# Two-layer diffusion backbone on one core: second layer's values with a column of ones, work taken off VectorE, output gate folded into the weights, first token tiles finished in an earlier turn

## The chip, the cores and the metric

The kernel runs on one core of a Trainium2 chip. The metric is the device time of one launch in microseconds (us). The instructions run on five engines: TensorE (PE in the profile; its weight loads are PEld), VectorE (DVE), ScalarE (ACT), GpSimd (POOL), and SyncE (SP), whose queue issues the DMA transfers.

## The reference

Two layers of a diffusion backbone over 1024 latent tokens and 256 context tokens of width 1024, and a final RMSNorm:

```python
for i in range(DEPTH):                                   # DEPTH = 2
    hx = rms_norm(x, norm_g[i]) * (1.0 + sc_x) + sh_x    # sh, sc, g: modulation from silu(c) @ w_mod[i]
    hc = rms_norm(ctx, norm_g[i]) * (1.0 + sc_c) + sh_c
    ...                                                  # layer 0: GQA, QK norm, rotary; layer 1: below
    x = x + g_x * yx
```

Layer 1 is a neighbourhood attention with 16 heads of width 64. A token sees a window of 8 rows by 16 columns of the 16 x 64 grid with a learned bias, and all context tokens:

```python
px = hx @ w_in                                           # q, k, v, z, each 1024 wide
s = concat([q @ k_window * ATTN_SCALE + bias, q @ k_ctx * ATTN_SCALE])
p = softmax(s)
o = p[..., :n_nb] @ v_window + p[..., n_nb:] @ v_ctx
yx = (o * silu(z)) @ w_out
```

The last layer gives no context output. The result is `rms_norm(x, final_norm_g)`.

## The kernel before, in words

**Precision.** Every product of two float32 matrices is done in float16 parts: a high part and a remainder of each factor (a "split"), and three matmuls (high x high, high x low, low x high). A split is a ScalarE copy to float16 and a VectorE or POOL subtraction.

**Stages.** Until about 136 us the modulation vectors are computed while weights arrive. Then comes layer 0 with its attention (names with a: `pa`, `pv`, `poa` are PSUM tiles of its projections, its weighted values and its out-projection), to about 774 us. Token tiles have 128 tokens: 0 to 7 are latent, 8 and 9 are context (NX = 8, NT = 10). Tile t's output is gated (`tm`, VectorE), added to the stream (`x1`, L1358, POOL) and handed to `ln_pair`, which normalises two tiles at once (`x16`, `x17` are tiles 6 and 7) and prepares layer 1's input.

**Entry of layer 1.** Its projections use a fast block multiplication (Winograd's form of Strassen: 7 block products for 8, `winograd`). So its factors are sums and differences of blocks, on the tokens' side made in `ln_pair` (L704 to L707: POOL, VectorE, POOL, VectorE) from the halves of a pair of tiles. The float16 rows before these sums are `hrb6a` for tiles 6 and 7, and after them `hrb6s` (`0` high, `1` low). DMA transposes them into `hx`. On the weights' side `b_load` forms the block sums (`wtb`, four POOL operations per weight tile, L1429 to L1432), and ScalarE and VectorE split them (`wb`, L1434, L1435). The products land in `pwq0a` to `pwq7c` (queries and keys of head pairs 0 to 7) and `pwv0a` to `pwv7c` (values and gates).

**Attention of layer 1.** `b_att(u)` works on head pair u: for each of 2 heads and 8 token tiles, scores over the near tiles and the context, a maximum, four exponentials (two into float16 `ph`, two into float32 `pf`, whose sums go into `bsm`), the remainder by `p_split` (every fourth on VectorE, L1127; the others as two halves on POOL, L1130), a DMA transposition into `bpht`, and then two matmuls per key tile (L1642 over 128 columns: values' high and low part at once; L1644 over 64). Per head and four tiles, `fin` (L1653 to L1660) makes the reciprocal of the sums, adds the two parts, scales and multiplies with the gate path `bsz`.

**Out-projection.** `b_part` multiplies with w_out; pairs 0 to 5 (K1 = 6) run during the last pair's attention, pairs 6 and 7 in `b_out(t)` (PSUM tiles `pob<t><half>6`). Each half-tile is multiplied with the gate (L1751, VectorE, `tmb`) and added to the residual `acc` (L1752, POOL, for tile 7 in `b_out` VectorE). Then `b_out` squares (L1760, ScalarE), takes the reciprocal root (L658 VectorE, L660 POOL) and scales (L1765, VectorE).

**What sets the order.** The program is written in the order that `timeline` makes from start and end values given to each part: of the live parts it takes a step of the one whose next step has the lowest value. Then `Planner` reorders each engine's instructions over the whole program, by a list schedule with its own costs and by due times derived from TensorE's order. So a change of one line can move instructions far from it.

## Time and profile before

| | us |
|---|---|
| median of three runs (lowest, highest) | 1360.35 (1357.03, 1361.37) |
| profiled execution | 1362.21 |
| its span | 1360.3 |
| busy: TensorE, VectorE, ScalarE, POOL | 1309.5, 1129.6, 976.2, 909.9 |

The mean granted clock of TensorE in the profiled execution is 0.991 of full. A busy time is the time in which at least one instruction of an engine was in flight. What is idle is told in the rows by the wait in square brackets and by what ended it.

### The profile page before, as it was taken

Reading aid. Unit: us, or ns where it says so; the run is one execution under the profiler, and the core shown is the slowest. Engines: PE = TensorE matmul, PEld = TensorE weight load, DVE = VectorE, ACT = ScalarE, POOL = GpSimd, SP = SyncE. Lnnn points to the kernel's source line nnn. Section 1 sums busy time; section 2 is a strip of 40 time slices with the busy share of each in tenths; the row PEclk is TensorE's granted clock in tenths of the full one; section 3 lists DMA queues with packets and bytes.
Section 4 is the critical chain, followed back from the end, with each engine's and each line's share of the span. In section 5 each row is a group of like instructions: output and inputs, shape, how many; then the busy total and the mean of one; then the engine's idle time right before and its main releaser. Section 6 shows DMA issues by size and latency. Waiting matters only on the chain.

```text
span 1360.3 us, 37879 instructions
## 1 busy us (share of the span) xinstructions
PE 1309.5 (96%) x14492; PEld 923.2 (68%) x14492; DVE 1129.6 (83%) x2603; ACT 976.2 (72%) x2325; POOL 909.9 (67%) x1251
## 2 busy tenths in 40 slices
PE   8999999999999999999999899999999999999994
PEld 4467777777777777776654357868677686876551
DVE  5898687978898787769448898899999999999668
ACT  4654889888888777788733355897978889787443
POOL 2323778777777767788775566586676778755565
PEclk9999999999999999999999999999999999999997
DMA  9634566787874222245237953587677768679953
GB/s 368 186 114 114 118 125 144 153 153 146 141 142 104 66 77 60 57 118 139 79 109 175 219 109 90 115 151 146 121 142 151 150 130 173 126 165 257 262 113 124
DMA packets 390350, 191.58 MB, mean 141 GB/s; under 512 B 349776, under 2 KB 355088, under 8 KB 390168
## 3 DMA queue, kind: packets, MB, share of 16 engines
q1 hardware_dynamic: 389592, 189.13, 61.6%
q8 instruction: 113, 1.85, 0.6%
q14 instruction: 69, 0.57, 0.1%
q10 hardware_dynamic: 576, 0.03, 0.0%
HBM read 91.03 MB, written 15.75 MB: 78 GB/s over the span
## 4 chain that ended last, share of the span: by engine, by line
PE 49%; DVE 24%; ACT 11%; issue 6%; DMA 5%; POOL 4%; DVEq 0%; POOLq 0%; SPq 0%; ACTq 0%
PE pa L1034 12%; PE pob L1747 5%; PE st L1260 3%; PE st L1261 3%; DVE wb L1435 3%; PE pm L1068 3%; PE poa L1353 2%; PE pv L1137 2%; PE pv L1136 2%; PE pv L1138 2%; DVE bpf L1613 2%; DVE bk L1504 2%; DVE bmx L1620 2%; ACT bpf L1633 1%; ACT bph L1631 1%
## 5 line engine op out<-in xcount | busy, mean ns | idle before, releaser
L1130 POOL TENSOR_TENSOR pl<-pf,ph 128x256 f16<-128x256 f32 x400 | 274.8, 712 | 83.3 <-ACT pf L1247 59.0
L1130 POOL TENSOR_TENSOR bph<-bpf,bph 128x256 f16<-128x256 f32 (+1 forms) x192 | 167.5, 889 | 119.0 <-ACT bpf L1633 98.7
L1034 PE MATMUL pa<-wa,x 128*128 128x256 f16 x1536 | 219.3, 272 | 1.0 <-DVE q L822 1.0
L1245 ACT ACTIVATE ph<-st 128x512 f16<-128x512 f32 x240 | 143.2, 602 | 56.4 <-PE st L1261 55.1
L1560 PEld LDWEIGHTS <-hx 128*128 128x128 f16 x2688 | 156.7, 98 | 11.7 <-issue 4.9
L1034 PEld LDWEIGHTS <-x 128*128 128x128 f16 x1536 | 139.7, 97 | 33.2 <-DVE q L822 1.3
L1247 ACT ACTIVATE pf<-st 128x512 f32<-128x512 f32 x240 | 143.2, 603 | 1.9 <-POOL pl L1130 1.2
L1069 DVE TENSOR_REDUCE mxp<-pm 128x1 f32<-128x512 f32 x192 | 127.5, 683 | 16.2 <-PE pm L1068 15.1
L1137 PE MATMUL pv<-v,ph 128*128 128x64 f16 x960 | 122.5, 195 | 0.0
L1136 PE MATMUL pv<-v,ph 128*128 128x65 f16 x960 | 122.1, 193 | 0.0
L1138 PE MATMUL pv<-v,pl 128*128 128x65 f16 x960 | 121.5, 192 | 0.4 <-POOL pl L1130 0.4
L1512 PEld LDWEIGHTS <-wb 128*128 128x128 f16 x672 | 63.5, 99 | 81.2 <-issue 10.9
L1130 POOL TENSOR_TENSOR qpp<-qpf,qpp 128x256 f16<-128x256 f32 (+1 forms) x158 | 94.2, 621 | 33.8 <-ACT qpf L1203 25.7
L1631 ACT ACTIVATE bph<-bpf,bnx 128x384 f16<-128x384 f32 (+1 forms) x128 | 69.9, 581 | 55.7 <-DVE bnx L1623 35.6
L1136 PEld LDWEIGHTS <-ph 128*128 128x128 f16 x960 | 90.7, 96 | 23.2 <-DVE og L1118 1.7
L1137 PEld LDWEIGHTS <-ph 128*128 128x128 f16 x960 | 90.3, 97 | 14.4 <-issue 0.4
L1138 PEld LDWEIGHTS <-pl 128*128 128x128 f16 x960 | 91.1, 99 | 9.4 <-POOL pl L1130 1.1
L1260 PE MATMUL st<-q,k 128*128 128x512 f16 x240 | 90.9, 379 | 1.9 <-ACT pf L1247 1.2
L1261 PE MATMUL st<-q,k 65*128 65x512 f16 x240 | 91.2, 381 | 0.0
L1353 PE MATMUL poa<-woa,oa 128*128 128x512 f16 x384 | 89.7, 379 | 0.0
L1747 PE MATMUL pob<-wob,obf 128*128 128x512 f16 x336 | 79.9, 379 | 0.2 <-DVE tmb L1751 0.2
L1633 ACT ACTIVATE bpf<-bpf,bnx 128x384 f32<-128x384 f32 (+1 forms) x128 | 74.4, 581 | 0.2
(486 smaller groups left out, 4045.6 us busy)
## 6 DMA issues: line engine op xcount, KB each, us to landing
wg<-in_w_mb SPq DMA_DIRECT2D x32, 512.0 KB
wsb<-in_b_wp SPq DMA_DIRECT2D x64, 256.0 KB
wm<-in_w_m SPq DMA_DIRECT2D x16, 512.0 KB
wsa<-in_a_wq SPq DMA_DIRECT2D x32, 256.0 KB
xstage<-in_x SPq DMA_DIRECT2D x8, 512.0 KB
wsoa<-in_a_w_out SPq DMA_DIRECT2D x16, 256.0 KB
x<-in_x SPq DMA_DIRECT2D x8, 512.0 KB
x_d<-x SPq DMA_DIRECT2D x8, 512.0 KB
```

Source lines behind the costliest of these rows:

```text
L1034: T.matmul(ps[:, :, i, :], hA(a, kt, t), wt[w][:, kt, :], start=n == 0, stop=n == 3 * KT - 1)
L1069: V.tensor_reduce(mxs[i][:, t, ch:ch + 1], pm, axis=AX.X, op=ALU.max)
L1130: G.tensor_tensor(lo[:, c], p32[:, c], hi[:, c], op=ALU.subtract)
L1136: T.matmul(pv[:, t, :], hi[:, c], v[:, 0:65], start=first and t == 0, stop=False)
L1137: T.matmul(pv[:, t, 0:HD], hi[:, c], v[:, 65:129], start=False, stop=False)
L1138: T.matmul(pv[:, t, :], lo[:, c], v[:, 0:65], start=False, stop=last and t == n - 1)
L1245: S.activation(ph, st, AF.Exp)
L1247: S.activation(p32, st, AF.Exp)
L1260: T.matmul(so, k1[:, g, kc], q1[:, :, i, :], start=True, stop=False)
L1261: T.matmul(so, k2[0:65, g, kc], q2[0:65, :, i, :], start=False, stop=True)
L1560: T.matmul(ps[:, t * P:(t + 1) * P], hx[a][:, t, blk, kt], wt[j][:, s_, w, kt], start=first and t == 0 and m == 0, stop=last and t == 3 an ...
L1747: T.matmul(ps, ob[kt][:, t, a], wout["b"][hf][b][:, kt, :], start=n == 0, stop=n == 3 * len(kts) - 1)
```

## The change

1. `p_split` in layer 1 gives every eighth remainder to VectorE instead of every fourth (BEV 4 to 8): 16 of 128 move to POOL, two instructions each.
2. `ln_pair`: of the four block sums three are now on VectorE and one on POOL, with one sign turned (`scalar_tensor_tensor` with -1). To keep the products right, the weights' blocks come in another order and `BLK` points to other blocks.
3. `load_wout` multiplies the second layer's w_out with the gate on POOL when a weight tile arrives (16 tiles of 128 x 512), so `b_part` adds from PSUM into `acc` on VectorE in one instruction; the gate tile of before and the POOL additions go.
4. The addition of `x1` for tile 7 of the first layer is on VectorE.
5. `b_load` forms its block sums with three POOL operations, one of them over 256 columns, instead of four.
6. The values of layer 1 have a column of 2*WS*WS beside the high part (tile 130 wide, set by a POOL memset per head pair). The exponentials no longer sum, and a key tile takes three matmuls of 65, 64 and 65 columns, with the denominator in column 64 of the result.
7. `fin` becomes `o_evict`, which the first layer uses too: a reciprocal from PSUM, a scaling in PSUM, a product with the gate path.
8. The copy of the queries in `put` (L1501, VectorE) is a second ScalarE write from PSUM.
9. In `b_out` the first half of tiles 0 to 6 is scaled on ScalarE and multiplied with the norm weight on POOL.
10. The parts have other values for their turn: the last pair's attention ends at u + 0.6, and `b_out(t)` starts at 7.61 (t < 4) or 7.65, plus 0.09 t, instead of 8.01 + 0.1 t.

```diff
-BEV, BLAG = 4, 4
+BEV, BLAG = 8, 4
...
-        G.tensor_tensor(b2, b1, b2, op=ALU.add)
-        V.tensor_tensor(b1, a1, b1, op=ALU.subtract)
-        G.tensor_tensor(a1, b2, a1, op=ALU.subtract)
+        V.scalar_tensor_tensor(b2, b1, -1.0, b2, op0=ALU.mult, op1=ALU.subtract)
+        G.tensor_tensor(b1, a1, b1, op=ALU.subtract)
+        V.scalar_tensor_tensor(a1, b2, -1.0, a1, op0=ALU.mult, op1=ALU.subtract)
         V.tensor_tensor(a2, a2, a1, op=ALU.subtract)
...
+                    if gate is not None:
+                        G.tensor_tensor(st, st, gw, op=ALU.mult)
                 load_w(w, f, kt, 1, 512, f"o{nm}{kt}{hf}")
...
-            G.tensor_tensor(x1[:, hc], x1[:, hc], tm, op=ALU.add)
+            (V if t == NX - 1 else G).tensor_tensor(x1[:, hc], x1[:, hc], tm, op=ALU.add)
...
-            G.tensor_tensor(t1, b12, b11, op=ALU.subtract)
-            G.tensor_tensor(t2, b22, t1, op=ALU.subtract)
-            G.tensor_tensor(t3, b22, b12, op=ALU.subtract)
+            G.tensor_tensor(tt[:, 0:2], st[:, 1:3], b12.unsqueeze(1).broadcast_to([P, 2, P]), op=ALU.subtract)
+            G.tensor_tensor(t2, b22, t1, op=ALU.add)
             G.tensor_tensor(t4, b21, t2, op=ALU.subtract)
...
-        v1_ = bq.tile([P, NT, 2, P], F16, name=f"bv1{u}", tag="v1")
+        v1_ = bq.tile([P, NT, 2, 130], F16, name=f"bv1{u}", tag="v1")
+        G.memset(v1_[:, :, :, HD:HD + 1], 2.0 * WS * WS)
...
-                    V.tensor_copy(ov[0][oth, i, ts], ov[0][own, i, ts])
+                    S.activation(ov[0][oth, i, ts], src, AF.Copy, scale=sc)
...
-                        S.activation(pf[:, 0:n], pf[:, 0:n], AF.Exp, bias=m, accum_out=sums[:, t % 4, 0:1])
-                        S.activation(pf[:, n:n + 2], cx_, AF.Exp, bias=m, accum_out=sums[:, t % 4, 1:2])
+                        S.activation(pf[:, 0:n], pf[:, 0:n], AF.Exp, bias=m)
+                        S.activation(pf[:, n:n + 2], cx_, AF.Exp, bias=m)
...
-                                T.matmul(pv[:, t % 4, :], pht[:, x_], v1_[:, kt, i, :], start=t % 4 == 0 and x_ == 0,
-                                         stop=False)
-                                T.matmul(pv[:, t % 4, 0:HD], plt[:, x_], v1_[:, kt, i, 0:HD], start=False,
+                                T.matmul(pv[:, t % 4, 0:65], pht[:, x_], v1_[:, kt, i, 0:65],
+                                         start=t % 4 == 0 and x_ == 0, stop=False)
+                                T.matmul(pv[:, t % 4, 0:HD], pht[:, x_], v1_[:, kt, i, 65:129], start=False, stop=False)
+                                T.matmul(pv[:, t % 4, 0:65], plt[:, x_], v1_[:, kt, i, 0:65], start=False,
                                          stop=t % 4 == 3 and x_ == len(keys) - 1)
...
-                    sm = bl.tile([P, 4], F32, name="bse" + nm, tag="bse", bufs=2)
-                    V.tensor_reduce(sm, sums, axis=AX.X, op=ALU.add)
-                    V.tensor_scalar_mul(sm, sm, 2.0 * WS * WS)
-                    V.reciprocal(sm, sm)
-                    oc = bl.tile([P, 4, HD], F32, name="boc" + nm, tag="boc", bufs=1)
-                    S.copy(oc, pv[:, :, HD:P])
-                    V.tensor_tensor(oc, pv[:, :, 0:HD], oc, op=ALU.add)
-                    V.tensor_tensor(oc, oc, sm.unsqueeze(2).broadcast_to([P, 4, HD]), op=ALU.mult)
-                    V.tensor_tensor(og[:, :, i * HD:(i + 1) * HD], oc, sz[:, hf * 4:hf * 4 + 4, i * HD:(i + 1) * HD],
-                                    op=ALU.mult)
+                    o_evict(bl, pv, og, 4, sz, hf * 4, i, f"b{u}{i}{hf}")
...
-        items.append((b_att(u), u, u + 1, C_BA))
+        items.append((b_att(u), u, u + (1 if u + 1 < NPAIR else 0.6), C_BA))
...
-        tm = bq.tile([P, 512], F32, name=f"tmb{t}{hf}{kts[0]}", tag="cc")
-        V.tensor_tensor(tm, ps, fin_c["g1"][:, hcs], op=ALU.mult)
-        eng.tensor_tensor(fin_c["acc"][t][:, hcs], fin_c["acc"][t][:, hcs], tm, op=ALU.add)
+        V.tensor_tensor(fin_c["acc"][t][:, hcs], ps, fin_c["acc"][t][:, hcs], op=ALU.add)
...
-            V.scalar_tensor_tensor(x2[:, hcs], x2[:, hcs], rs[:, 0:1], fg[:, hcs], op0=ALU.mult, op1=ALU.mult)
+            if hf or t == NX - 1:
+                V.scalar_tensor_tensor(x2[:, hcs], x2[:, hcs], rs[:, 0:1], fg[:, hcs], op0=ALU.mult, op1=ALU.mult)
+            else:
+                S.activation(x2[:, hcs], x2[:, hcs], AF.Copy, scale=rs[:, 0:1])
+                G.tensor_tensor(x2[:, hcs], x2[:, hcs], fg[:, hcs], op=ALU.mult)
...
-        items.append((b_out(t), 8.01 + 0.1 * t, 8.11 + 0.1 * t, 2560))
+        v = (7.61 if t < 4 else 7.65) + 0.09 * t
+        items.append((b_out(t), v, v + 0.09, 2560))
```

The planner writes every engine's order anew. At two places the prediction rests on it. The first is VectorE between the statistics of token tile 7 (`lssb6b`) and the rows of tiles 6 and 7; `tm80` is the gated out-projection of context tile 8, `wb000` the first split weights of layer 1. Before:

```order
L658 TENSOR_SCALAR ms_ln_14266<-lssb6b_14264 128x1
L677 SCALAR_TENSOR_TENSOR x16_14056<-x16_14056,rs_ln_14258,lrow10_13846 128x512
L690 TENSOR_TENSOR hrb4s1_14150<-x14_13892,hrb4s0_14149 128x512
L678 TENSOR_TENSOR x16_14056<-x16_14056,lrow00_13844 128x512
L677 SCALAR_TENSOR_TENSOR x17_14161<-x17_14161,rs_ln_14268,lrow10_13846 128x512 x2
L678 TENSOR_TENSOR x17_14161<-x17_14161,lrow00_13844 128x512 x2
L677 SCALAR_TENSOR_TENSOR x16_14056<-x16_14056,rs_ln_14258,lrow10_13846 128x512
L690 TENSOR_TENSOR hrb6a1_14253<-x17_14161,hrb6a0_14252 128x512
L678 TENSOR_TENSOR x16_14056<-x16_14056,lrow00_13844 128x512
L690 TENSOR_TENSOR hrb6a1_14253<-x16_14056,hrb6a0_14252 128x512
L705 TENSOR_TENSOR x17_14161<-x16_14056,x17_14161 128x512
L690 TENSOR_TENSOR hrb6a1_14253<-x16_14056,hrb6a0_14252 128x512
```

After, on the same engine at the same place:

```order
L658 TENSOR_SCALAR ms_ln_14266<-lssb6b_14264 128x1
L677 SCALAR_TENSOR_TENSOR x16_14056<-x16_14056,rs_ln_14258,lrow10_13846 128x512 x2
L678 TENSOR_TENSOR x16_14056<-x16_14056,lrow00_13844 128x512 x2
L677 SCALAR_TENSOR_TENSOR x17_14161<-x17_14161,rs_ln_14268,lrow10_13846 128x512 x2
L678 TENSOR_TENSOR x17_14161<-x17_14161,lrow00_13844 128x512 x2
L690 TENSOR_TENSOR hrb6a1_14253<-x16_14056,hrb6a0_14252 128x512
L690 TENSOR_TENSOR hrb6a1_14253<-x17_14161,hrb6a0_14252 128x512
L690 TENSOR_TENSOR hrb6a1_14253<-x16_14056,hrb6a0_14252 128x512
L704 SCALAR_TENSOR_TENSOR x17_14161<-x17_14161 128x512
L1362 TENSOR_TENSOR tm80_14249<-poa80_14224,gt8_14220 128x512
L1439 SCALAR_TENSOR_TENSOR wb000_14356<-wsb000_14358,wb000_14356 128x3x128
L706 SCALAR_TENSOR_TENSOR x16_14056<-x17_14161,x16_14056 128x512
```

The three splits of `hrb6a` now stand together ahead of the pair's first block sum, where before the last of them stood behind a block sum (L705).

The second is VectorE at the end of the program; `pob706` and `pob716` are the last out-projection banks of tile 7, `rs_fin` the reciprocal root of a tile, `fss50` a tile's sum of squares. Before:

```order
L1751 TENSOR_TENSOR tmb706_24533<-pob706_24526,g1_23366 128x512
L1751 TENSOR_TENSOR tmb716_24545<-pob716_24538,g1_23366 128x512
L1765 SCALAR_TENSOR_TENSOR acc_23352<-acc_23352,rs_fin_24413,fg_23378 128x512 x2
L1765 SCALAR_TENSOR_TENSOR acc_23352<-acc_23352,rs_fin_24448,fg_23378 128x512 x2
L1761 TENSOR_TENSOR fss50_24454<-fss50_24454,fss51_24455 128x1
L1761 TENSOR_TENSOR fss60_24489<-fss60_24489,fss61_24490 128x1
L1752 TENSOR_TENSOR acc7_23353<-acc7_23353,tmb706_24533 128x512
L658 TENSOR_SCALAR ms_fin_24481<-fss50_24454 128x1
L658 TENSOR_SCALAR ms_fin_24516<-fss60_24489 128x1
L1752 TENSOR_TENSOR acc7_23353<-acc7_23353,tmb716_24545 128x512
L1765 SCALAR_TENSOR_TENSOR acc_23352<-acc_23352,rs_fin_24483,fg_23378 128x512 x2
L1765 SCALAR_TENSOR_TENSOR acc_23352<-acc_23352,rs_fin_24518,fg_23378 128x512 x2
```

After:

```order
L1742 TENSOR_TENSOR acc_23682<-pob606_24835,acc_23682 128x512
L1756 SCALAR_TENSOR_TENSOR acc_23682<-acc_23682,rs_fin_24794,fg_23706 128x512
L1751 TENSOR_TENSOR fss50_24801<-fss50_24801,fss51_24802 128x1
L1742 TENSOR_TENSOR acc_23682<-pob616_24845,acc_23682 128x512
L658 TENSOR_SCALAR ms_fin_24824<-fss50_24801 128x1
L1742 TENSOR_TENSOR acc7_23683<-pob706_24867,acc7_23683 128x512
L1751 TENSOR_TENSOR fss60_24833<-fss60_24833,fss61_24834 128x1
L1756 SCALAR_TENSOR_TENSOR acc_23682<-acc_23682,rs_fin_24826,fg_23706 128x512
L658 TENSOR_SCALAR ms_fin_24856<-fss60_24833 128x1
L1742 TENSOR_TENSOR acc7_23683<-pob716_24877,acc7_23683 128x512
L1756 SCALAR_TENSOR_TENSOR acc_23682<-acc_23682,rs_fin_24858,fg_23706 128x512
L1751 TENSOR_TENSOR fss70_24865<-fss70_24865,fss71_24866 128x1
```

Between tile 7's last reading of PSUM and its sum of squares VectorE had 14 instructions before, eight of them scalings of tiles 3 to 6 over 512 columns; now it has one scaling, of tile 6.

More of the change, by code (lines that the diff above doesn't have):

```diff
@@ L1290, in trunk_kernel, with load_wout @@
     wout = {}
-    def load_wout(src, nm):
+    def load_wout(src, nm, gate=None):
         ws = []
@@ L1297, in load_wout @@
             ws.append(w)
+            if gate is not None:
+                gw = bl.tile([P, 512], F32, name=f"gw{hf}", tag="gw", bufs=1)
+                DM.dma_start(gw, gate[:, hf * 512:(hf + 1) * 512].broadcast_to([P, 512]))
             for kt in range(KT):
@@ L1300, in f @@
                     DM.dma_start(st, src[kt * P:(kt + 1) * P, hf * 512:(hf + 1) * 512])
+                    if gate is not None:
+                        G.tensor_tensor(st, st, gw, op=ALU.mult)
                 load_w(w, f, kt, 1, 512, f"o{nm}{kt}{hf}")
@@ L1426, in b_load @@
             DM.dma_start(st, b_wp[u, kind, kt])
-            b12, b11, b21, b22 = (st[:, j] for j in range(4))
-            t1, t2, t3, t4 = (tt[:, j] for j in range(4))
-            G.tensor_tensor(t1, b12, b11, op=ALU.subtract)
-            G.tensor_tensor(t2, b22, t1, op=ALU.subtract)
-            G.tensor_tensor(t3, b22, b12, op=ALU.subtract)
+            b12, b11, b22, b21 = (st[:, j] for j in range(4))
+            t1, t3, t2, t4 = (tt[:, j] for j in range(4))
+            G.tensor_tensor(tt[:, 0:2], st[:, 1:3], b12.unsqueeze(1).broadcast_to([P, 2, P]), op=ALU.subtract)
+            G.tensor_tensor(t2, b22, t1, op=ALU.add)
             G.tensor_tensor(t4, b21, t2, op=ALU.subtract)
@@ L1521, in ctx_k @@
                 for a, b in ((0, 0), (0, 1), (1, 0)):
-                    T.matmul(ps[:, 0:NC * P].rearrange("p (t q) -> p t q", q=P), wt[0][:, kt // 4, a, kt % 4],
+                    T.matmul(ps[:, 0:NC * P].rearrange("p (t q) -> p t q", q=P), wt[0][:, kt // 4 * 2, a, kt % 4],
                              hc[b][:, :, kt], start=m == 0, stop=m == 3 * KT - 1)
@@ L1571, in ctx_v @@
                     for a, w in ((0, 0), (0, 1), (1, 0)):
-                        T.matmul(ps[:, t * P:(t + 1) * P], hc[a][:, t, kt], wt[0][:, kt // 4, w, kt % 4],
+                        T.matmul(ps[:, t * P:(t + 1) * P], hc[a][:, t, kt], wt[0][:, kt // 4 * 2, w, kt % 4],
                                  start=t == 0 and m == 0, stop=t == NC - 1 and m == 3 * KT - 1)
@@ L1600, in b_att @@
                 pv = psum.tile([P, 4, P], F32, name=f"bpv{u}{i}{hf}", tag="pv", bufs=2)
-                sums = bl.tile([P, 4, 2], F32, name=f"bsm{u}{i}{hf}", tag="sums", bufs=2)
                 for t0 in (hf * 4, hf * 4 + 2):
@@ L1731, in b_open @@
                     ob[u] = obf[:, u]
-            if not u0:
-                fin_c["g1"] = y_tile((P, D), F32, "g1", 0)
-                DM.dma_start(fin_c["g1"], gate_d[1, 0:1, :].broadcast_to([P, D]))
         for t in range(NX):
@@ L1757, in b_out @@
         for hf in range(2):
-            yield from b_part(t, hf, range(K1, NPAIR), "st", V if t == NX - 1 else G)
+            yield from b_part(t, hf, range(K1, NPAIR), "st")
             jk = bq.tile([P, 512], F32, name=f"jk{t}{hf}", tag="th", bufs=1)
@@ L1770, in trunk_kernel @@
         for t in range(NX):
[L1771 to L1772 removed]
+            v = 7.03 + 0.058 * (NX * hf + t)
+            items.append((b_part(t, hf, range(K1), "pj"), v, v + 0.058, 640 * K1))
     for t in range(NX):
[L1774 removed]
+        v = (7.61 if t < 4 else 7.65) + 0.09 * t
+        items.append((b_out(t), v, v + 0.09, 2560))
     run_all(timeline(items))
@@ L1824 @@
         "a_w_out": i["a_w_out"][0],
-        "b_wp": np.stack([np.stack([wb[h, :, :, r] for h, r in ((0, r2), (0, r1), (1, r1), (1, r2))], 2)
+        "b_wp": np.stack([np.stack([wb[h, :, :, r] for h, r in ((0, r2), (0, r1), (1, r2), (1, r1))], 2)
                           for r1, r2 in ((1, 0), (2, 3))]).transpose(4, 0, 1, 2, 3, 5),
```

13 lines of the change are left out of this document (5 added, 8 removed).

## The prediction

> **What bounds the kernel now.** I read the busy time by stage first (start; first layer; where its output enters the second layer; second layer's attention; the out-projection after the last attention; what follows the last matmul), then TensorE's waits and timeline, and last the engines that it waits for. The first table's columns are the stretch, its length, each engine's busy time with its instruction count, TensorE's granted clock, the DMA share and the rate.
>
> ```profile
> 0.00:136.00 136.00, 126.86 (x891) 76.63 (x892) 110.55 (x278) 70.01 (x147) 41.76 (x57) 1.00 0.62 196
> 136.00:774.00 638.00, 632.33 (x7545) 449.57 (x7544) 492.18 (x1174) 484.18 (x1048) 473.34 (x671) 1.00 0.55 121
> 774.00:830.00 56.00, 48.58 (x501) 33.59 (x499) 51.59 (x76) 25.46 (x46) 36.14 (x52) 0.91 0.56 119
> 830.00:1258.00 428.00, 417.57 (x5038) 320.67 (x5036) 404.38 (x946) 354.29 (x968) 299.11 (x417) 1.00 0.74 149
> 1258.00:1342.50 84.50, 83.92 (x526) 42.73 (x523) 58.05 (x111) 37.93 (x107) 54.61 (x49) 1.00 0.65 159
> 1342.50:1360.30 17.80, 0.22 (x2) 0.00 (x0) 12.90 (x25) 4.33 (x12) 4.93 (x7) 0.57 0.55 206
> ```
>
> TensorE (first busy column) is idle 9.1 us at the start, 5.7 in the first layer, 7.4 at the entry, 10.4 in the second layer's attention, 0.6 in the out-projection, and then 17.6 of the last 17.8 while others finish. It is the bound everywhere but in that tail. So a change can win there, at the entry and in the waits of the attention, and each matmul it adds costs its full cadence. VectorE is close behind in the attention: 404 of 428 us.
>
> **1. The weighted sum of values.** Before, a key of a head takes two matmuls, of 128 and 64 columns; after, three, of 65, 64 and 65, with the denominator in column 64. The layer has 608 keys (22 near keys and 16 context keys in each of 16 heads), so 608 matmuls more. The first layer already has the shape of after. The timeline has both (start, busy, engine, line, tiles, shapes):
>
> ```profile
> 524.55 0.19 PE L1136 MATMUL pv<-v,ph 128*128 128x65 f16 x1
> ...
> 524.92 0.27 PE L1034 MATMUL pa<-wa,x 128*128 128x256 f16 x1
> ```
> ```profile
> 1096.21 0.22 PE L1642 MATMUL bpv<-bv,bpht 128*128 128x128 f16 x1
> ...
> 1096.55 0.22 PE L1560 MATMUL pwv5a<-wb,hx 128*128 128x128 f16 x1
> ```
>
> From the first row to the last lie 12 matmuls (four keys) in the first layer, 0.37 us, or 92.5 ns a key; in the second eight (four keys), 0.34 us, or 85. The third matmul so adds 7.5 ns a key: 608 x 7.5 ns = **+4.6 us**, all on TensorE's path. The ends are +2 and +8, since the starts are rounded to 10 ns. Against it speaks the Trainium skill, "TensorE: Matmul & The Clock Gate", section "Back-to-back issue gap": a sustained stream of weight load and matmul runs at about 81 ns each at 128 columns. By that page 608 more such pairs would cost an estimated 49 us; the rows of four keys contradict it at 31 ns each.
>
> **2. The entry of the second layer.** Its first projection needs the normalised rows of token tiles 6 and 7, split in two halves and transposed by DMA (hrb6a for the tiles themselves, hrb6s for their sums).
>
> ```profile
> 753.78 20.88 PE L1353 MATMUL poa<-woa,oc 128*128 128x512 f16 x96
> 778.28 0.39 PE L1512 MATMUL pwq0a<-hx,wb 128*128 128x512 f16 x1 [3.62 <-DMA hx<-hrb6a]
> 779.58 4.85 PE L1512 MATMUL pwq0a<-hx,wb 128*128 128x512 f16 x11 [0.90 <-DMA hx<-hrb6a]
> ```
> ```profile
> 764.04 0.14 DVE L658 TENSOR_SCALAR ms_ln<-lssb6b 128x1 f32<-128x1 f32 x1
> ...
> 771.45 0.68 DVE L690 TENSOR_TENSOR hrb6a<-x,hrb6a 128x512 f16<-128x512 f32 x1
> 773.28 0.69 DVE L705 TENSOR_TENSOR x<-x,x 128x512 f32<-128x512 f32 x1 [1.16 <-POOL x L704]
> 773.89 0.68 DVE L690 TENSOR_TENSOR hrb6a<-x,hrb6a 128x512 f16<-128x512 f32 x1
> ```
> ```profile
> 757.53 1.26 POOL L1358 TENSOR_TENSOR x<-x,tm 128x512 f32<-128x512 f32 x1
> ...
> 771.00 2.25 POOL L704 TENSOR_TENSOR x<-x 128x512 f32<-128x512 f32 x1 [4.42 <-DVE hrb6a L690]
> ```
> ```profile
> 762.02 1.05 ACT L673 ACTIVATE hrb6a<-x 128x1024 f16<-128x1024 f32 x1
> ```
> ```profile
> 780.00:784.00 4.00, 4.00 (x11) 1.43 (x10) 4.00 (x7) 0.52 (x1) 2.96 (x4) 0.50 1.09 223
> ```
>
> The last matmuls of the first layer end at 753.78 + 20.88 = 774.66; then TensorE waits 3.62 and 0.90 us, and its clock falls to 0.50. The stretch 774 to 830 has clock 0.91, so 0.09 x 56 = 5.0 us more are lost. Together 9.5.
>
> The last split of hrb6a ends at 774.57, and the first wait ends 3.7 later. That split stands behind L705, which waits for a POOL subtraction of 2.25 us. After, the order of VectorE has the three splits ahead of any subtraction of this pair, L704 and L706 are on VectorE (0.69 for such an op) and wait for POOL nowhere, and tile 7's addition follows on VectorE. Between lssb6b at 764.04 and the end are now 11 instructions of about 0.65: 7.2 us instead of 10.5, so at least 3.3 earlier. The statistics lssb6b themselves can come 4 us earlier: the POOL addition ends at 758.8 and only a squaring need follow, which runs from 762.02 for 1.05, behind other work. Hrb6a is then split by 767 to 771 and lands by 771 to 775, about when the cover of 96 matmuls ends. Late next is hrb6s, whose last split is nine instructions (6 us) behind: it lands at 777 to 781, while pwq0a (24 matmuls of 0.216, the spacing of a 512-column matmul in the out-projection rows of part 4) occupies TensorE until 780. So 1 to 2.5 us of wait remain: **-7 us**, ends -9.5 and 0 (the planner's new order makes something else late).
>
> Whether the 5.0 goes hangs on the hole that remains. Waits of up to 1.3 us (next part) leave the clock at 1.00; 3.62 does not. Between them the trace shows nothing. The Trainium skill, same page, section "Part 1: The HAM clock gate", puts the clock to half after an idle window of about 3.4 us; by that rule a hole of 2.5 keeps full clock and the term stays -7, by the rows alone it could be -2 there.
>
> **3. Waits in the attention.**
>
> ```profile
> PE pwv7c L1560 <- DVE bv L1542: 1.3, 1, 1.3
> PE pwq6b L1512 <- DVE w2q L1465: 1.2, 1, 1.2
> PE bpv L1642 <- DMA bpht<-bph: 1.0, 1, 1.0
> ```
> ```profile
> L1501 DVE COPY bq<-bq 64x512 f16<-64x512 f16 x28 | 14.7, 534 | 0.7
> L1127 DVE TENSOR_TENSOR bph<-bpf,bph 128x512 f16<-128x512 f32 (+1 forms) x27 | 24.6, 912 | 0.6 <-ACT bpf L1634 0.3
> L1654 DVE TENSOR_SCALAR bse<-bse 128x4 f32<-128x4 f32 x28 | 12.1, 434 | 0.0
> L1658 DVE TENSOR_TENSOR boc<-bpv,boc 128x256 f32<-128x256 f32 x27 | 11.2, 415 | 0.8 <-ACT boc L1657 0.7
> ```
> ```profile
> L1634 ACT ACTIVATION_READ_ACCUMULATOR bpf<-bsc,bnx 128x1 f32 x112 | 22.6, 201 | 0.0
> L1633 ACT ACTIVATION_READ_ACCUMULATOR bpf<-bpf,bnx 128x1 f32 x112 | 21.6, 193 | 0.0
> L1657 ACT COPY boc<-bpv 128x256 f32<-128x256 f32 x28 | 10.3, 369 | 0.2
> ```
> ```profile
> L1130 POOL TENSOR_TENSOR bph<-bpf,bph 128x256 f16<-128x256 f32 (+1 forms) x168 | 147.8, 897 | 105.7 <-ACT bpf L1633 94.2 <-ACT bpf L1634 10.8 <-POOL bph L1130 0.3
> L1429 POOL TENSOR_TENSOR wtb<-wsb 128x128 f32<-128x128 f32 x46 | 30.3, 658 | 7.9 <-DMA wsb<-in_b_wp 3.7 <-DVE wb L1435 3.1 <-DVE bsz L1551 1.0
> ```
>
> Waits give us in total, times and longest; groups give busy us, mean ns, and idle time before. VectorE loses the copies (14.7), half its splits (12) and, at each head's end, L1654, L1658 and a reduction (some 27): about 54 of its 404 us. ScalarE loses 44 of accumulator reads and 10 of copies, and gains 28 writes over 512 columns, at the 0.63 that one takes in part 4: 17.5. POOL gains 14 splits of two 0.9 us halves (+25) and 16 gate multiplications (128x512; 1.26 each as L1358 in part 2, +20), and loses an operation and half its overhead per weight tile (46 x 0.4, -18): 299 becomes 326 of 428, with 106 us of its idle before the splits spent on ScalarE, which is relieved. The eight memsets of 128x20 I cost at nothing, as POOL has that idle. So waits on VectorE shrink, and what is late next are probabilities on POOL and their transpose (the third wait). Of 10.4 us I take **-3**; ends -10 (all) and +4 (as many waits on POOL as were on VectorE).
>
> **4. The end.**
>
> ```profile
> 1341.91 0.81 PE L1747 MATMUL pob<-wob,ob 128*128 128x512 f16 x3
> ```
> ```profile
> 1346.84 2.72 DVE L1765 SCALAR_TENSOR_TENSOR acc<-acc,rs_fin,fg 128x512 f32<-128x512 f32 x4
> ...
> 1350.35 0.68 DVE L1752 TENSOR_TENSOR acc<-acc,tmb 128x512 f32<-128x512 f32 x1
> 1351.46 2.74 DVE L1765 SCALAR_TENSOR_TENSOR acc<-acc,rs_fin,fg 128x512 f32<-128x512 f32 x4 [0.44 <-POOL rs_fin L660]
> ...
> 1355.19 1.42 DVE L1765 SCALAR_TENSOR_TENSOR acc<-acc,rs_fin,fg 128x512 f32<-128x512 f32 x2 [0.73 <-POOL rs_fin L660]
> ```
> ```profile
> 1351.21 0.63 ACT L1760 ACTIVATE jk<-acc 128x512 f32<-128x512 f32 x1
> 1351.74 0.19 ACT L1760 ACTIVATION_READ_ACCUMULATOR jk<-acc 128x1 f32 x1
> ```
>
> The last matmuls start every 0.22 us until 1342.5. VectorE then works off a queue: the scalings of tiles 3 and 4 stand ahead of tile 7's last addition, which ends at 1351.0, 8.5 us later, and those of tiles 5 and 6 ahead of its statistics. After, every tile has one addition from PSUM per half (0.69) and one scaling (0.7), about 2.4 us with the small ones, against six matmuls a half, 2.6 us a tile: VectorE keeps up. Left are the last addition 0.7, squaring 0.8 (ScalarE's two rows), statistics and POOL's power 1.0 (from 1354.2, where the four scalings end, to 1355.2 before), two scalings 1.4, the store 3.7 (1356.6 to 1360.3): 7.6, and up to 2.5 for tile 6's half through ScalarE and POOL (1.3), whose POOL part stands ahead of the power. So 10 for 17.8: **-7**, being cautious by 1; ends -9 and -2. The gate multiplications on VectorE and the 30 additions on POOL that go ran under TensorE until then, so beyond this queue they give nothing.
>
> **5. The rest.** The other order of the weight blocks reads the same bytes with the same matmuls. That the out-projection's tiles 0 to 3 take their turn earlier adds no instruction; what it is worth is in part 4's queue. The planner writes the first layer's order anew with the same matmuls; its idle of 5.7 us bounds the gain, and I take 0 with +-3.
>
> **Sum:** 4.6 - 7 - 3 - 7 + 0 = -12.4. The profiled execution took 1362.2 (span 1360.3 and 1.9 around it), so 1349.8; the median of the runs shown is 1.9 lower: **1348 us**.
>
> **Rivals.** *All waits go*: entry -9.5, attention -8, tail -9, with +4.6 make -22, 1338. For it: VectorE falls from 404 to about 350 of 428, and no other engine is above 0.85. Against: the first layer too keeps 5.7. *Something else covers the relief*: the entry stays at 0 because another chain (hrb6s) reopens a hole over 3 us and with it the half clock, the attention stays at 0, and the tail gives 4: +0.6, about 1359 to 1361, within. *POOL becomes the bound*: each of the 16 splits that move (14 of them in the stage of part 3) is followed by a wait of TensorE for the transposed probabilities as long as the longest seen, 1.0: +16, with the entry at -4 and the tail at -2 and the 4.6 this is +14.6, 1375; half of that wait gives 1367. With the entry and tail so, it decides (slower by 4) from 0.35 us at each moved split. POOL's 326 of 428 speaks against. *The page's rule on weight loads*: 1348 + 44 = 1392.
>
> **How the numbers follow.** Chances: my forecast 0.58, all waits go 0.17, covered 0.15, POOL the bound 0.09, weight loads 0.01. The range is from the second case, 1338, to 1359, the near edge of the third; it leaves out about 2 in 10. A measurement of this kernel tells about 0.3% from no change, 4 us: 1356.3 to 1364.4. The first two cases lie below it, with a little of the first's upper end inside; so faster 0.75, same 0.15, slower 0.10.
>
> **What the profile after would show.** For part 1: four keys in 0.37 us, and TensorE's time of that stage up by 4 to 5 less waits. For part 2: the wait on hrb6a under 1.5 us, and a clock of 0.98 or more from 774 to 830. For part 3: VectorE at about 350 of 428, waits on it under 4 us, POOL near 326. For part 4: 9 to 11 us after the last matmul, the last addition within 1.5 of it. I would be wrong if a hole of over 3 us stays before the first projection, if TensorE waits for transposed probabilities more than a few us in all, or if ScalarE and POOL delay the last tile's power.

## The result

The changed kernel takes 1344.65 us (median of 4 runs, 1343.26 to 1345.52), the kernel before 1359.9 beside it: a ratio of 0.9886 with a 95% interval of 0.9874 to 0.9899, some 15 us less. The prediction was 1348 in a range of 1338 to 1359. The profiled execution has a span of 1343.7 us against 1360.3.

Cut at three marks of the program (the last matmul of the first layer, 56 us behind it, the last matmul of all), the busy times by stage are these; columns as in the prediction's first table. Before:

```profile
0.00:774.70 774.70, 759.86 (x8436) 526.30 (x8436) 603.43 (x1452) 554.84 (x1195) 515.75 (x728) 1.00 0.56 134
774.70:830.70 56.00, 48.61 (x503) 34.12 (x504) 51.59 (x77) 25.52 (x47) 35.49 (x52) 0.91 0.55 117
830.70:1342.70 512.00, 500.99 (x5555) 362.76 (x5553) 461.93 (x1052) 391.52 (x1073) 353.92 (x467) 1.00 0.72 151
1342.70:1360.30 17.60, 0.02 (x1) 0.00 (x0) 12.70 (x25) 4.33 (x12) 4.73 (x7) 0.57 0.55 204
```

After:

```profile
0.00:774.40 774.40, 761.77 (x8437) 527.86 (x8438) 611.35 (x1467) 557.61 (x1197) 507.66 (x720) 0.99 0.56 136
774.40:830.40 56.00, 51.54 (x542) 37.24 (x541) 49.91 (x79) 30.17 (x57) 37.36 (x48) 0.97 0.43 109
830.40:1333.10 502.70, 496.31 (x6124) 363.48 (x6122) 400.62 (x905) 379.26 (x820) 342.32 (x443) 1.00 0.76 157
1333.10:1343.70 10.60, 0.00 (x0) 0.00 (x0) 5.27 (x8) 2.00 (x5) 3.82 (x4) 0.61 0.41 154
```

The first layer ends as before (-0.3). From there to the last matmul it is 558.7 us instead of 568.0 (-9.3), and behind the last matmul 10.6 instead of 17.6 (-7.0). Of the -9.3, the third matmul per key costs +4.7 (below). So waits and half clock give -14.0: at the entry 6.3 (idle 7.4 to 4.5 us; lost to the clock 5.0 to 1.7, which is 0.09 and 0.03 of 56), and behind it the remaining 7.7. Of these 7.7 the busy times show only 4.6 as idle (11.0 to 6.4), since the record of a matmul is longer than the spacing to the next (0.19 us against 0.03 in the weighted sum) and covers part of a delay. Counted from start to start, TensorE's delays behind the entry (over 50 ns beyond the usual spacing of a shape) fall from 15.9 us (34 of them) to 8.3 (12), so by 7.6.

The entry after, in TensorE's and VectorE's timelines:

```profile
774.21 2.75 PE L1517 MATMUL pwq0a<-hx,wb 128*128 128x512 f16 x12
777.96 1.24 PE L1517 MATMUL pwq0a<-hx,wb 128*128 128x512 f16 x5 [1.00 <-ACT e1q L1457]
...
788.21 0.81 PE L1517 MATMUL pwq0b<-hx,wb 128*128 128x512 f16 x3 [2.15 <-DVE w1q L1461]
```
```profile
758.64 0.14 DVE L658 TENSOR_SCALAR ms_ln<-lssb6b 128x1 f32<-128x1 f32 x1
...
763.78 1.89 DVE L690 TENSOR_TENSOR hrb6a<-x,hrb6a 128x512 f16<-128x512 f32 x3
...
786.68 0.87 DVE L690 TENSOR_TENSOR hrb<-x,hrb 128x512 f16<-128x512 f32 x1
787.48 0.68 DVE L1461 TENSOR_TENSOR w1q<-e1q,pwq0b 128x512 f32<-128x512 f32 x1
```

The rows of tiles 6 and 7 are split at 765.7 instead of 774.6, and the first projection follows the first layer without a hole. What TensorE waits for now is w1q, which stands on VectorE behind the normalising of the context tiles.

From 830 to 1258 us the waits on VectorE fall from 6.9 us to 2.1 (1.4 of them in the out-projection), and the transposed probabilities lead. The waits up to 1332, and the stage's busy times, after:

```profile
PE bpv L1646 <- DMA bpht<-bph: 3.5, 5, 1.0
PE pob L1739 <- DVE acc L1742: 1.4, 1, 1.4
PE pob L1739 <- DVE ms_fin L658: 0.6, 1, 0.6
PE pwv3c L1565 <- DVE bnx L1626: 0.4, 1, 0.4
```
```profile
830.00:1258.00 428.00, 422.21 (x5572) 324.74 (x5571) 353.62 (x811) 341.28 (x733) 306.25 (x406) 1.00 0.78 157
```

### The profile page after: what moved, and what is told of

Read it like the earlier page. It is cut to its first block, busy times and chain, and to the rows that moved or that the text cites. A ratio compares the mean times of both kernels' runs of the same rounds, so it can differ in the third digit from the quotient of the medians.

```text
span 1343.7 us, 38645 instructions
## 1 busy us (share of the span) xinstructions
PE 1309.6 (97%) x15100; PEld 928.6 (69%) x15100; DVE 1067.1 (79%) x2456; ACT 969.0 (72%) x2076; POOL 891.2 (66%) x1214
## 4 chain that ended last, share of the span: by engine, by line
PE 73%; DVE 10%; ACT 6%; DMA 5%; issue 3%; POOL 2%; DVEq 0%; POOLq 0%; SPq 0%; ACTq 0%
PE pa L1034 13%; PE poa L1358 6%; PE pob L1739 6%; PE st L1260 3%; PE st L1261 3%; PE pm L1068 3%; PE pkv L887 2%; PE pv L1137 2%; PE pv L1138 2%; PE pv L1136 2%; DMA bpht<-bph 2%; DMA qpp<-qpp 2%; PE pvc L1577 1%; PE qpv L1211 1%; PE pbc L1527 1%
## 5 line engine op out<-in xcount | busy, mean ns | idle before, releaser
L1130 POOL TENSOR_TENSOR bph<-bpf,bph 128x256 f16<-128x256 f32 (+1 forms) x224 | 184.0, 848 | 102.0 <-ACT bpf L1637 81.8
L1565 PEld LDWEIGHTS <-hx 128*128 128x128 f16 x2688 | 157.3, 98 | 10.2 <-issue 1.3
L1434 POOL TENSOR_TENSOR wtb<-wsb 128x256 f32<-128x256 f32 x64 | 56.5, 884 | 32.5 <-DMA wsb<-in_b_wp 17.0
```

Of the source, the lines that this page charges most:

```text
L1130: G.tensor_tensor(lo[:, c], p32[:, c], hi[:, c], op=ALU.subtract)
L1565: T.matmul(ps[:, t * P:(t + 1) * P], hx[a][:, t, blk, kt], wt[j][:, s_, w, kt], start=first and t == 0 and m == 0, stop=last and t == 3 an ...
```

## The experiments

A sum over all runs first, read from the same three marks. "Middle" is from the last matmul of the first layer to the last of all, "end" what follows. Each ratio is to the kernel before as measured beside that run (medians of 1359.9 to 1361.1 us), so two runs are best compared by their ratios; 0.001 is 1.4 us. Stages come from one profiled execution each.

| run | median us | ratio to before (95%) | first layer ends | middle | end |
|---|---|---|---|---|---|
| before | 1359.9 | 1 | 774.7 | 568.0 | 17.6 |
| after | 1344.65 | 0.9886 (0.9874 to 0.9899) | 774.4 | 558.7 | 10.6 |
| after, once more (e4) | 1345.36 | 0.9886 (0.9871 to 0.9902) | 771.6 | 559.2 | 10.7 |
| before + entry (e1) | 1362.51 | 1.0011 (1.0003 to 1.002) | 779.1 | 563.7 | 17.6 |
| the same, old first-layer order (e5) | 1356.02 | 0.9963 (0.9951 to 0.9975) | 775.1 | 560.8 | 18.3 |
| before + ones (e2) | 1373.17 | 1.0091 (1.0078 to 1.0105) | 780.3 | 574.0 | 17.7 |
| the same, old first-layer order (e6) | 1369.25 | 1.006 (1.0047 to 1.0072) | 773.2 | 576.0 | 18.3 |
| after, old turns (e3) | 1348.01 | 0.9904 (0.989 to 0.9917) | 775.0 | 561.1 | 10.1 |
| after, splits and copies back (e7) | 1349.71 | 0.9918 (0.9906 to 0.9929) | 773.1 | 563.0 | 10.8 |
| after, gate and scaling back (e8) | 1352.16 | 0.9935 (0.9921 to 0.9948) | 775.8 | 561.9 | 14.9 |
| after, ones back (e9) | 1354.56 | 0.9959 (0.9946 to 0.9973) | 773.2 | 569.7 | 10.6 |
| the same, own buffer (e12) | 1357.54 | 0.9985 (0.9976 to 0.9994) | 773.6 | 568.7 | 10.2 |
| after, no split on VectorE (e10) | 1346.15 | 0.99 (0.9884 to 0.9917) | 772.0 | 560.8 | 10.8 |
| after, copies back (e11) | 1350.45 | 0.993 (0.9909 to 0.9952) | 771.6 | 562.0 | 10.3 |

### The entry alone (e1, then e5)

The kernel before with the edits of `ln_pair`, `a_out`, `b_load` and `BLK` (points 2, 4 and 5 of the change):

```diff
-        G.tensor_tensor(b2, b1, b2, op=ALU.add)
-        V.tensor_tensor(b1, a1, b1, op=ALU.subtract)
-        G.tensor_tensor(a1, b2, a1, op=ALU.subtract)
+        V.scalar_tensor_tensor(b2, b1, -1.0, b2, op0=ALU.mult, op1=ALU.subtract)
+        G.tensor_tensor(b1, a1, b1, op=ALU.subtract)
+        V.scalar_tensor_tensor(a1, b2, -1.0, a1, op0=ALU.mult, op1=ALU.subtract)
...
```

> The kernel before with the entry's edits alone (block sums of ln_pair on VectorE, tile 7's addition on VectorE, three POOL operations per weight tile). My theory, that the hole before the first projection is its own loss and closes with these: 6 us less than before, about 1354, with the clock at full until 780 and a wait on hrb6a under 1 us. The rival, that VectorE was late there because of work that the other edits take off it: within 2 us of before, and a hole of over 2 us on hrb6a.

Neither number came: 1.4 us slower, though the hole had closed and the clock stayed full there. The middle is 4.3 us shorter, but the first layer, which but for one addition no edit of these touches, ends 4.4 us later. The planner makes six orders and keeps the one that its own estimate likes best: for the kernel before the last, for this one the fourth. So a second run kept the same pass:

```diff
-        self.order = best[1]
```

> The entry's edits alone again, as in the run of the entry only, but with the planner's last pass kept, so that the first layer's instructions stand in the same order as before on TensorE, VectorE, POOL and SyncE. If the entry closes its hole and the loss of the first run lay in the first layer's new order: the first layer ends within 2 us of 774.3, and 4 to 6 us less than before, about 1356. If what the entry gives is given back behind it: 1360 to 1362.

It gave 1356.02 against 1360.62, the first layer ends at 775.1, and the middle is 7.2 us shorter. Its stage behind the first layer:

```profile
775.10:831.10 56.00, 50.76 (x542) 36.75 (x540) 52.12 (x83) 27.80 (x53) 34.58 (x47) 1.00 0.48 102
```

Idle 5.2 instead of 7.4, and 5.0 of clock regained: the entry's edits are worth 4.6 us (times) to 7.2 us (middle) by themselves. What hid it in the first run was the planner's order: of the 6.5 us between the two runs 4.0 lie in the first layer, whose work the edits hardly touch, and 2.9 in the middle.

### The column of ones alone (e2, then e6)

The kernel before with points 6 and 7:

```diff
-        v1_ = bq.tile([P, NT, 2, P], F16, name=f"bv1{u}", tag="v1")
+        v1_ = bq.tile([P, NT, 2, 130], F16, name=f"bv1{u}", tag="v1")
+        G.memset(v1_[:, :, :, HD:HD + 1], 2.0 * WS * WS)
...
+                    o_evict(bl, pv, og, 4, sz, hf * 4, i, f"b{u}{i}{hf}")
```

> The kernel before with the column of ones alone (three matmuls per key, exponentials without sums, the short ending of a head). If TensorE's waits in the second layer's attention follow the load of VectorE and ScalarE, which lose some 30 and 54 us: 4.7 us more matmul time less 3 to 4 of waits, 1360 to 1362. If these waits are single late chains that the load does not move: 4.7 more than before, about 1365, waits as before (10 us from 830 to 1258).

12 us slower, more than either. Again the first layer ends later (780.3), so a second run, with the last pass kept:

> The column of ones alone again, with the first layer in the same order as before. If the edit itself costs its 4.7 us of matmuls and no more, and the rest of the 12 us lay in the first layer's order: 1365 to 1367. If the edit makes the second layer's weights late (the waits of 4 us on wb at the entry): 1369 or more, with the first layer as before.

8.6 us slower with the first layer as before: the second expectation. In both, TensorE waits at the entry, where this edit adds no instruction but a memset, for the split weights wb, in e6 twice 3.3 us and in e2 twice 4 us. In e2:

```profile
785.80 3.17 PE L1513 MATMUL pwq0a<-hx,wb 128*128 128x512 f16 x7 [4.21 <-DVE wb L1435]
...
800.69 1.05 PE L1513 MATMUL pwq0b<-hx,wb 128*128 128x512 f16 x3 [4.08 <-DVE wb L1435]
```

So alone the column costs its matmuls, and some 3 to 4 us more by another order at the entry; the idle time in the attention shrinks little (8.4 us from 830 to 1258 in e6, against 10.4), and 5.8 us of it are now waits for the transposed probabilities. Why the planner puts the weights later there was not tried.

### The column undone in the changed kernel (e9, e12)

Points 6 and 7 undone, with the planner's first refining pass kept, as for the changed kernel. In e9 the ending's scratch tile had to share a buffer with another tile; in e12 it has its own.

```diff
-                    o_evict(bl, pv, og, 4, sz, hf * 4, i, f"b{u}{i}{hf}")
+                    V.tensor_reduce(sm, sums, axis=AX.X, op=ALU.add)
+                    V.tensor_scalar_mul(sm, sm, 2.0 * WS * WS)
...
```

> The changed kernel with the column of ones undone (two matmuls per key, sums of the exponentials on ScalarE, the long ending of a head), the first layer's order unchanged. The ending's scratch tile lies in another buffer, for room. If the column pays by the relief of VectorE and ScalarE: TensorE has 4.7 us less of matmuls, and waits grow by as much or more: 1345 or slower, with over 9 us idle from 830 to 1258. If the column only costs: 1340 to 1342, a kernel faster than the changed one.

> The changed kernel with the column of ones undone again, the ending's scratch tile now in a buffer of its own as before the change (the gate tile lies in a buffer of the projections instead, free when the gate is needed). If the 10 us of the first such run are what the column gives beside the other edits: 1352 or more, with 15 us or more of waits after the entry. If they came from the shared scratch buffer: 1340 to 1347.

The middle grows by 10 to 11 us although TensorE has 4.7 us less to do; the shared buffer was not the reason. Both first expectations came: TensorE is idle 10.4 us from 830 to 1258 in e9, and 17.2 us behind the entry in e12. The waits of e12 from 830 to 1340, and its busy times behind the entry:

```profile
PE bsn L1597 <- DVE bmx L1617: 3.8, 3, 1.9
PE bsc L1597 <- ACT bpf L1638: 3.7, 3, 1.7
PE bpv L1646 <- DMA bpht<-bph: 2.4, 3, 0.8
PE pwq2a L1516 <- ACT e1q L1457: 1.1, 1, 1.1
```
```profile
829.60:1342.30 512.70, 495.46 (x5518) 359.21 (x5515) 436.10 (x1003) 413.26 (x1110) 350.14 (x437) 1.00 0.74 154
```

ScalarE, which got the copies and final scalings, is at 413 of 513 us (379 of 503 after), VectorE at 436 (401). TensorE's scores wait for the maxima and for the exponentials. So the column costs 8.6 us in the old kernel and gives 10 to 13 in the new one (medians of e9 and e12; the profiled execution of e12 was its fastest), where it makes room on ScalarE and VectorE beside the other edits. Which of those needs that room was not separated.

### Splits and copies back (e7), copies alone (e11), no split on VectorE (e10)

All with the changed kernel's first-layer order.

```diff
-BEV, BLAG = 8, 4
+BEV, BLAG = 4, 4
...
-                    S.activation(ov[0][oth, i, ts], src, AF.Copy, scale=sc)
+                    V.tensor_copy(ov[0][oth, i, ts], ov[0][own, i, ts])
```

> The changed kernel with every fourth split and the copies of the queries back on VectorE (27 us of work), the first layer's order unchanged. If TensorE's waits in the attention shrank because VectorE has less to do: 3 to 6 us slower than the changed kernel, 1348 to 1351, and 9 us or more of idle TensorE from 830 to 1258. If they shrank because ScalarE lost its accumulator reads and a head's ending its chain: within 1.5 us of the changed kernel.

> The changed kernel with the copies of the queries back on VectorE alone (17 us of work to VectorE, 17 off ScalarE). If the 4.6 us that copies and splits together gave went with VectorE's load: 2 to 3 us slower than the changed kernel, 1347 to 1348. If they were the splits alone: within 1 us.

e7 is 5 us slower (4.4 by the ratios), its middle 4.3 longer: the first expectation, though TensorE's idle time from 830 to 1258 is 8.0 us and not 9. The copies alone (the second edit only) make the middle 3.3 longer in the profile, which is the fastest of six executions. Their median, 1350.45, is even above that of both together, and the times scatter from 1346.1 to 1354.3: more than that the copies bear a part isn't shown, and for the splits not even that.

```diff
-BEV, BLAG = 8, 4
+BEV, BLAG = 1 << 20, 4
```

> The changed kernel with all splits of the second layer on POOL (none on VectorE instead of every eighth), the first layer's order unchanged. If TensorE's waits follow VectorE's load: 1 to 2 us faster, 1343 to 1344. If POOL becomes the bound, as my slower rival had it: waits on the transposed probabilities over 6 us (3.5 in the changed kernel) and 2 us or more slower.

Neither: 1346.15 against 1344.65 and 1345.36 for the changed kernel, the same within these runs' scatter, the middle 1.6 to 2.1 longer. POOL rises to 328 of 428 us, and the wait that the slower rival needed shrinks:

```profile
830.00:1258.00 428.00, 422.47 (x5567) 324.13 (x5566) 353.74 (x796) 341.79 (x734) 327.82 (x434) 1.00 0.78 158
```
```profile
PE pwq6c L1517 <- DVE bk L1509: 0.9, 1, 0.9
...
PE bpv L1646 <- DMA bpht<-bph: 0.6, 3, 0.3
```

### Old turns (e3), gate and scaling back (e8)

```diff
-            items.append((b_out(t), v, v + 0.09, 2560))
+        items.append((b_out(t), 8.01 + 0.1 * t, 8.11 + 0.1 * t, 2560))
...
```

> The changed kernel with the old turns alone (last attention to u + 1, b_out at 8.01 + 0.1 t, steps of 0.06). If the short tail comes from the earlier turn of the first token tiles: 4 to 6 us slower than the changed kernel, about 1350, with 15 us or more after the last matmul. If it comes from the instructions that VectorE loses there: within 1.5 us of the changed kernel, 11 us after the last matmul.

3 us slower, 2.4 by the ratios, whose intervals touch; neither expectation in full. It is not at the end: 10.1 us follow the last matmul. What the turns are worth is in the middle (2.4 longer), where TensorE waits twice for VectorE's addition instead of once, 1.1 us more:

```profile
PE pob L1739 <- DVE acc L1742: 2.5, 2, 1.4
```

```diff
-        V.tensor_tensor(fin_c["acc"][t][:, hcs], ps, fin_c["acc"][t][:, hcs], op=ALU.add)
+        V.tensor_tensor(tm, ps, fin_c["g1"][:, hcs], op=ALU.mult)
+        eng.tensor_tensor(fin_c["acc"][t][:, hcs], fin_c["acc"][t][:, hcs], tm, op=ALU.add)
...
-            if hf or t == NX - 1:
+            if True:
```

> The changed kernel with the gate multiplied on VectorE and added on POOL again in the out-projection, and all final scalings on VectorE; the turns stay new and the first layer's order unchanged. If the short end comes from VectorE's fewer instructions: 4 to 7 us slower than the changed kernel, 1349 to 1352, with 14 us or more after the last matmul. If the earlier turns make it: within 1.5 us, with 11 us after the last matmul.

7 us slower, the first expectation: the end takes 14.9 (+4.3) and the middle 561.9 (+3.2). VectorE's timeline has the old picture, scalings ahead of the last tile's addition:

```profile
1335.78 4.74 DVE L1761 SCALAR_TENSOR_TENSOR acc<-acc,rs_fin,fg 128x512 f32<-128x512 f32 x4
...
1341.91 0.68 DVE L1747 TENSOR_TENSOR acc<-acc,tmb 128x512 f32<-128x512 f32 x1
1342.51 2.73 DVE L1761 SCALAR_TENSOR_TENSOR acc<-acc,rs_fin,fg 128x512 f32<-128x512 f32 x4
1345.16 0.68 DVE L1747 TENSOR_TENSOR acc<-acc,tmb 128x512 f32<-128x512 f32 x1
```

### Another plan (e4)

```diff
-        plan.refine(5, 100.0, 300.0)
+        plan.refine(4, 100.0, 300.0)
```

> The changed kernel with four passes of the planner's refinement in place of five: the same instructions, in another order on every engine. It measures what a new order is worth by itself. If the terms of the change are what they seem: within 2 us of the changed kernel (1342.6 to 1346.6). If the gain is mostly an order that happened to be good: 4 us or more slower.

It became another thing than was expected: the planner had kept its first refining pass in both, so this is the changed kernel once more, instruction for instruction. It serves as a measure of scatter: 1345.36 against 1344.65, but 2.2 us between the profiled spans; the first layer alone differs by 2.8 (771.6 and 774.4). Over all nine profiles with this first-layer order that layer ends between 771.6 and 775.8. What one profile shows of a stage is good to about 2 us either way.

## Why the prediction came out, step by step

**The weighted sum** (+4.6): right. Fifteen matmuls, five keys, after:

```profile
1096.15 0.19 PE L1646 MATMUL bpv<-bv,bpht 128*128 128x65 f16 x1
...
1096.61 0.27 PE L1565 MATMUL pwv5b<-wb,hx 128*128 128x128 f16 x2
```

0.46 us, 92 ns a key. Over all launches of these lines the spacing, delays left out, is 56.3 us after and 51.6 before, +4.7. The Trainium skill's 81 ns for each pair of weight load and matmul at 128 columns ("TensorE: Matmul & The Clock Gate", section "Back-to-back issue gap") is not borne out here: these pairs take 31 ns at 64 or 65 columns, and the 2688 launches of L1565, at 128 columns and with a weight load each, a median of 56 ns.

**The entry** (-7, ends -9.5 and 0): right in mechanism and nearly in size, -6.3 in the profile and -4.6 to -7.2 alone. Two steps were off. The next late thing is not hrb6s (its wait is nowhere) but w1q behind the context tiles' normalising, which the part did not look at. And the rule that the prediction took from the Trainium skill ("TensorE: Matmul & The Clock Gate", section "Part 1: The HAM clock gate"), by which a hole of 2.5 keeps the full clock, did not hold: in the profiled execution the 2.15 us on w1q were followed by 3.4 us at half clock (last section). The term did not suffer: in the repeat (e4) the clock stays full at the entry, but TensorE is idle 6.1 us there instead of 4.5, so idle time and lost clock together are 6.1 and 6.2.

**Waits in the attention** (-3, ends -10 and +4): the term that was mis-sized: -7.7 by the marks, inside its range but more than twice the value taken. The step that was off is the weight given to "what is late next are probabilities on POOL". They are late next, but cost 3.5 us in all, and POOL with still more work (e10) costs no more. What the term lacked is a price for the relief of ScalarE and VectorE together: with both loaded again (e12) the waits come back on the exponentials and the maxima. The loads behind it were partly off. VectorE came to 354 of 428 us as forecast (about 350). POOL came to 306, not 326: only eight of the 16 gate multiplications fall in this stretch (12 us, not 20), the splits add 19 instead of 25, and the block sums give 21.5 instead of 18. ScalarE fell by 13 us, not by the 36.5 that 44, 10 and 17.5 make: a read of the accumulator starts 0.1 us before the activation ahead of it ends (1351.74 against 1351.84 in the prediction's rows), so half of each read was covered already. Of the relief, splits and copies bear about 4 us (e7), gate and scalings about 3 (e8). Together with the column these parts make more than the term; that each undoes the room of another would explain it, but was not tried. The entry's edits were not undone in the changed kernel.

**The end** (-7): -7.0, and for the reason given. Fewer instructions on VectorE make most of it (e8 gives back 4.3; the other 2.7 were not separated); the turns alone don't (e3: 10.1). VectorE's last addition ends 0.8 us behind the last matmul, not 8.5:

```profile
1332.43 0.16 DVE L1751 TENSOR_TENSOR fss<-fss,fss 128x1 f32<-128x1 f32 x1 [0.19 <-ACT jk L1750]
1332.51 0.74 DVE L1756 SCALAR_TENSOR_TENSOR acc<-acc,rs_fin,fg 128x512 f32<-128x512 f32 x1
...
1333.24 0.68 DVE L1742 TENSOR_TENSOR acc<-pob,acc 128x512 f32<-128x512 f32 x1
1334.05 1.75 DVE L1756 SCALAR_TENSOR_TENSOR acc<-acc,rs_fin,fg 128x512 f32<-128x512 f32 x1
1335.72 1.21 DVE L1751 TENSOR_TENSOR fss<-fss,fss 128x1 f32<-128x1 f32 x1
1336.96 0.15 DVE L658 TENSOR_SCALAR ms_fin<-fss 128x1 f32<-128x1 f32 x1
1337.85 1.42 DVE L1756 SCALAR_TENSOR_TENSOR acc<-acc,rs_fin,fg 128x512 f32<-128x512 f32 x2 [0.73 <-POOL rs_fin L660]
```
```profile
1333.98 1.26 POOL L1759 TENSOR_TENSOR acc<-acc,fg 128x512 f32<-128x512 f32 x1
1335.42 1.49 POOL L1759 TENSOR_TENSOR acc<-acc,fg 128x512 f32<-128x512 f32 x1 [0.18 <-ACT acc L1758]
1337.26 0.55 POOL L660 TENSOR_TENSOR rs_fin<-ms_fin,mhalf 128x1 f32<-128x1 f32 x1 [0.35 <-DVE ms_fin L658]
```

The 2.5 us that the prediction allowed for tile 6's half were spent, but not on POOL alone: beside POOL's two multiplications VectorE's scaling took 1.75 us instead of 0.74 and its small addition 1.21 instead of 0.16, some 2 us ahead of the last power. So moving that half to ScalarE and POOL may have cost time here; what the end would be without it was not tried.

**The first layer** (0, +-3): -0.3 here, with 10.2 us at half clock in the first 66; the repeat has none and ends it at 771.6. But e1 and e2 had orders that ended it at 779.1 and 780.3. That the term was nought is luck of the pass that the planner kept; an honest range for it would have been -3 to +6.

**The rivals.** POOL as the bound is refuted by e10, and the price of a weight load by the +4.7. "All waits go" (1338) did not come: TensorE is still idle 10.9 us between the first layer and the last matmul, against 18.4 before. "Something else covers the relief" did happen to single edits: to the entry alone (e1), by the first layer's order, and to the ones alone (e6), at the entry.

The sum, -12.4, came to -16.6 of span; the waits, 4.7 beyond the forecast, make the difference, less 0.7 at the entry.

## What to carry to other kernels

Where a planner rewrites every order, compare edits with the order of the untouched part held fixed: two edits here looked 6 and 4 us worse than with the old pass of the planner kept, mostly because that part had moved. An edit's worth depends on the others: the column of ones lost 8.6 us alone and won 10 to 13 beside the edits that load the engine it relieves, so cost each relieved engine together with what is moved onto it. At the end of a kernel, read the queue of the engine that finishes it, instruction by instruction.

## What the runs showed of the hardware

**The clock gate.** The same wait, 2.15 us for w1q in the same program, was followed by half clock in the profiled execution of the changed kernel and by none in its repeat (e4). The stretches are the hole, what follows to the drop, and the next 3.4 us. After:

```profile
786.00:788.20 2.20, 0.05 (x1) 0.00 (x0) 2.20 (x5) 1.69 (x3) 2.20 (x4) 1.00 0.00 0
788.20:789.40 1.20, 1.20 (x7) 0.60 (x7) 1.20 (x2) 0.63 (x1) 0.18 (x1) 0.99 1.41 117
789.40:792.80 3.40, 3.39 (x11) 1.31 (x10) 2.95 (x6) 1.66 (x3) 0.00 (x0) 0.50 0.53 115
```

The repeat:

```profile
783.10:785.40 2.30, 0.16 (x1) 0.00 (x0) 2.30 (x5) 1.77 (x3) 2.30 (x4) 1.00 0.00 0
785.40:786.60 1.20, 1.19 (x7) 0.59 (x7) 1.20 (x2) 0.63 (x1) 0.19 (x1) 1.00 1.23 118
786.60:790.00 3.40, 2.03 (x12) 0.91 (x11) 3.40 (x7) 1.66 (x3) 0.00 (x0) 1.00 0.52 115
```

The drop comes when TensorE is busy again, so it looks like a fixed window that is judged at its end. The traces bear this out: where one has several half-clock stretches, their starts lie whole multiples of 3.413 us apart (789.38 is 214 of them behind one at 58.93 and 160 ahead of one at 1335.52). On this grid the window ahead of the drop, and the least busy one around the same wait in the repeat (its grid counted back from its only drop, at 1334.52), are:

```profile
785.97:789.38 3.41, 1.26 (x8) 0.58 (x7) 3.41 (x6) 2.35 (x4) 2.41 (x4) 1.00 0.49 41
```
```profile
781.57:784.98 3.41, 1.69 (x8) 0.68 (x7) 3.41 (x6) 1.67 (x3) 3.41 (x5) 1.00 0.00 0
```

TensorE is busy for 0.37 of the first and 0.50 of the second, which holds only a part of the hole. In the 14 traces, from 70 us to the last matmul, half clock goes with that share: of the windows at full clock all eleven at 0.40 or below were followed by it, two of the seven from 0.43 to 0.46 were, and none of the thousands above. So by where it falls on the grid the same hole brings half clock or not. The Trainium skill ("TensorE: Matmul & The Clock Gate", section "Part 1: The HAM clock gate") has the free-running window of about 3.4 us, which agrees with the length of the drop, but an idle window as the cause; here 2.15 idle us were enough in one execution and not in another.

**VectorE beside POOL.** With no split on VectorE (e10) it has 15 instructions less than after from 830 to 1258 and is busy as long, 353.7 and 353.6 us, while POOL is busy 22 us more: VectorE's other instructions took longer. The changed kernel's trace has the pattern from 830 to 1258 us. An instruction of VectorE that runs beside POOL's for more than half its time takes longer when its data lie in SBUF (the split of `wtb`, L1439: 965 ns against 725; `bnx`, L1627: 391 against 160), and as long as otherwise when it reads PSUM (`bmx` from `bsc`, L1624: 683 against 685; the scaling of `bpv` in `o_evict`, L1116: 424 against 423). In the old ending of a head the scaling in SBUF (L1659) took 612 against 418, so the new one, which works in PSUM, also escapes this. That the two engines hold each other up was not tried by itself.
